# One critical section with hand-kept semaphores and a hardware loop on TensorE, in a batched A x B-transposed matmul

## Chip, cores and metric

The kernel runs on one core of one Trainium2 chip. The metric is the device time of one execution in microseconds (us). Nine runs of the kernel before have a median of 126.72 us, from 126.57 to 126.99 us.

## The reference

Sixteen independent products of a 512 x 512 matrix with the transpose of another, all in float32:

```python
batch, m, k, n = 16, 512, 512, 512
a: (batch, m, k) float32      b: (batch, n, k) float32
out = np.matmul(a, b.transpose(0, 2, 1)).astype(np.float32)
```

33.55 MB are read from HBM and 16.78 MB are written. TensorE (PE) contracts over the partition dimension, and both operands have k as their last dimension, so both must be turned before they can be multiplied.

## The kernel before

Batches are handled in pairs. Of a pair, 128 partitions hold the two batches, 64 partitions each; a partition holds eight consecutive rows of 512 floats, which is one run of 16 KB in HBM. J = 4 is the number of 128-row blocks of a batch, KO = 4 that of 128-wide blocks of k, HP = 64.

The work of a pair goes through five steps.

1. `load` (issued on SP's queue): one DMA for a and one for b, 2 MiB each (L56). The last pair is loaded in four DMAs of 1 MiB, batch by batch, in 8 KB runs (L50).
2. `halve`: VectorE (DVE) casts the loaded tile to bf16 in two pieces of 128 x 2048 (L64).
3. `turn_pair`: for each of the four ko, PE transposes eight 128 x 128 blocks into one PSUM tile `tp` by multiplying with an identity (L72). ScalarE (ACT) copies the a tiles to SBUF in two strided pieces (L78), DVE copies the b tiles in one (L85). All four ko of a come first, then all four of b; `tp` has four buffers. The last pair uses `turn_single` (L97, L102) batch by batch.
4. `multiply`: for each batch, four groups of four matmuls of 128 x 512 accumulate over ko in a PSUM tile `ps` (L111); ACT copies each to the output tile `o_sb` (L115).
5. `store`: one DMA of 1 MiB per batch on SP's queue (L122), in 8 KB runs.

The order is written out by hand: three pairs are loaded ahead; then, in the program of each engine, pair u's casts, transposes, matmuls and two stores are followed by the loads of pair u + 3. The framework places the semaphores that this order needs. SP's queue holds loads and stores in one line, so a store that waits for its output tile holds back the loads that stand behind it. PE's program is unrolled over all sixteen batches: 512 transposes and 256 matmuls, each with a weight load of its own.

Of the kernel before, what the change touches and what calls it, by code (L numbers as in the profile page):

```python
# [1 line left out]

# [5 lines left out]


@with_exitstack  # L10
def kernel(
    ctx: ExitStack,
    tc: tile.TileContext,
    a: bass.AP,
    b: bass.AP,
    out: bass.AP,
):
    nc = tc.nc
    P = 128
    batch, M, K = a.shape  # L20
    _, N, _ = b.shape
    J = M // P
    KO = K // P
    HP = P // 2
    f32 = mybir.dt.float32
    bf16 = mybir.dt.bfloat16
    AHEAD = 3

    const = ctx.enter_context(tc.tile_pool(name="ident", bufs=1))
    ident = const.tile([P, P], bf16)  # L30
    make_identity(nc, ident)

    apool = ctx.enter_context(tc.tile_pool(name="a_pool", bufs=3))
    bpool = ctx.enter_context(tc.tile_pool(name="b_pool", bufs=3))
    hpool = ctx.enter_context(tc.tile_pool(name="h_pool", bufs=3))
    tpool = ctx.enter_context(tc.tile_pool(name="t_pool", bufs=2))
    opool = ctx.enter_context(tc.tile_pool(name="o_pool", bufs=6))
    tppool = ctx.enter_context(tc.tile_pool(name="tp_pool", bufs=4, space=bass.MemoryType.PSUM))
    ppool = ctx.enter_context(tc.tile_pool(name="p_pool", bufs=4, space=bass.MemoryType.PSUM))

    def load(u, split):
        a_sb = apool.tile([P, 2 * J, K], f32, tag="a")
        b_sb = bpool.tile([P, 2 * J, K], f32, tag="b")
        if split:
            for e in range(2):
                for dst, src in ((a_sb, a), (b_sb, b)):
                    nc.sync.dma_start(  # L50
                        dst[:, e * J:(e + 1) * J, :],
                        src[2 * u + e].rearrange("(p j) k -> p j k", j=J),
                    )
        else:
            for dst, src in ((a_sb, a), (b_sb, b)):
                nc.sync.dma_start(  # L56
                    dst[:],
                    src[2 * u:2 * u + 2].rearrange("e (p j) k -> (e p) j k", j=2 * J),
                )
        return a_sb, b_sb  # L60

    def halve(src, e, tag):
        half = hpool.tile([P, J, K], bf16, tag="h" + tag)
        nc.vector.tensor_copy(out=half[:], in_=src[:, e * J:(e + 1) * J, :])  # L64
        return half

    def turn_pair(halves, is_a):
        turned = tpool.tile([P, KO, 2 * J * P], bf16, tag="ta" if is_a else "tb")
        for ko in range(KO):
            tp = tppool.tile([P, 2 * J, P], bf16, tag="tp")  # L70
            for j in range(2 * J):
                nc.tensor.transpose(  # L72
                    tp[:, j, :], halves[j // J][:, j % J, ko * P:(ko + 1) * P], ident[:]
                )
            if is_a:

                for e in range(2):
                    nc.scalar.copy(  # L78
                        out=turned[:, ko, e * J * P:(e + 1) * J * P].rearrange(
                            "k (j p h) -> k j p h", j=J, h=2  # L80
                        ),
                        in_=tp[:, :, e * HP:(e + 1) * HP].rearrange("k (h j) p -> k j p h", h=2),
                    )
            else:
                nc.vector.tensor_copy(  # L85
                    out=turned[:, ko, :], in_=tp[:].rearrange("k j p -> k (j p)")
                )
        return turned

    def turn_single(half, is_a):  # L90
        turned = tpool.tile([P, KO, J * P], bf16, tag="ta" if is_a else "tb")
        copy = nc.scalar.copy if is_a else nc.vector.tensor_copy
        for ko in range(0, KO, 2):
            tp = tppool.tile([P, 2, J * P], bf16, tag="tp")
            for h in range(2):
                for j in range(J):
                    nc.tensor.transpose(  # L97
                        tp[:, h, j * P:(j + 1) * P],
                        half[:, j, (ko + h) * P:(ko + h + 1) * P],
                        ident[:],  # L100
                    )
            copy(out=turned[:, ko:ko + 2, :], in_=tp[:])  # L102
        return turned

    def multiply(aT, bT, groups):

        o_sb = opool.tile([P, J, N], f32, tag="o")
        for j in range(J):
            ps = ppool.tile([P, N], f32, tag="p")
            for ko in range(KO):  # L110
                nc.tensor.matmul(  # L111
                    ps[:], aT(ko, j), bT(ko), start=(ko == 0), stop=(ko == KO - 1)
                )

            nc.scalar.copy(  # L115
                out=o_sb[:, j, :].rearrange("m (p j) -> m p j", j=groups),
                in_=ps[:].rearrange("m (j p) -> m p j", j=groups),
            )
        return o_sb

    def store(i, o_sb):
        nc.sync.dma_start(out[i].rearrange("(p j) n -> p j n", j=J), o_sb[:])  # L122

    pairs = batch // 2
    loaded = {}
    with tc.manual_schedule():
        for u in range(AHEAD):
            loaded[u] = load(u, u == pairs - 1)
        for u in range(pairs):
            a_sb, b_sb = loaded.pop(u)  # L130
            if u < pairs - 1:
                a_h = [halve(a_sb, e, "a") for e in range(2)]
                b_h = [halve(b_sb, e, "b") for e in range(2)]
                aT = turn_pair(a_h, True)
                bT = turn_pair(b_h, False)
                for e in range(2):
                    o_sb = multiply(
                        lambda ko, j: aT[:, ko, (e * J + j) * P:(e * J + j + 1) * P],
                        lambda ko: bT[:, ko, :].rearrange("k (j p) -> k j p", j=2 * J)[
                            :, :, e * HP:(e + 1) * HP  # L140
                        ],
                        2 * J,
                    )
                    store(2 * u + e, o_sb)
            else:
                for e in range(2):
                    a_h = halve(a_sb, e, "a")
                    b_h = halve(b_sb, e, "b")
                    aT = turn_single(a_h, True)
                    bT = turn_single(b_h, False)  # L150
                    o_sb = multiply(
                        lambda ko, j: aT[:, ko, j * P:(j + 1) * P],
                        lambda ko: bT[:, ko, :],
                        J,
                    )
                    store(2 * u + e, o_sb)
            if u + AHEAD < pairs:
                loaded[u + AHEAD] = load(u + AHEAD, u + AHEAD == pairs - 1)


# [1 line left out]
_INS = ['a', 'b']  # L162
_OUTS = [((16, 512, 512), 'float32')]


# [23 lines left out]
```

## Time and profile before

| | |
|---|---|
| median of 9 runs | 126.72 us (126.57 to 126.99) |
| profiled execution, its own time | 126.71 us |
| its span, first to last instruction | 124.9 us |
| granted TensorE clock, mean | 0.984 |
| busy: PE, weight loads, DVE, ACT | 94.3, 58.4, 58.7, 70.2 us |
| data on the DMA queues | 50.33 MB, 96.2% of 16 engines' span |
| HBM traffic over the span | 403 GB/s |

The page gives busy times of each engine over the span, and the span in 40 equal slices with a digit for the busy tenths of each; the DMA row is the mean busy share of 16 DMA engines, and GB/s is what they moved. "out<-in" names the tiles by the program's names. A group of instructions is told with its busy time, the mean of one, and the idle time of the engine ahead of it with what ended it. In the timeline the columns are the start, the duration, the engine and line, the operation, its tiles and shapes, the number of instructions and in brackets the idle time before. In the windows there stand, after the length, the busy time of each engine, the granted clock of PE, the DMA share and GB/s.

### The profile page before, as it was taken

The page shows a single profiled execution, that of the slowest core. Times are in us where ns is not written, and L with a number is a line of the kernel's source. Part 1 is how long each engine was busy: PE and PEld are TensorE (multiplying, and loading weights), DVE is VectorE, ACT ScalarE, POOL GpSimd, SP SyncE. Part 2 cuts the span into 40 slices and gives each one's busy share as a digit, 9 for nine tenths or more (in the row PEclk, how much of TensorE's full clock was granted, in tenths as well). Part 3 has the DMA queues.
Part 4 walks back from the last instruction along what each step waited for, and adds up shares of the span by engine and source line. Part 5 has one row for each costly group of instructions (what it writes and reads, how often), then busy time and mean ns, then how long its engine had stood idle before and what let it go on. Part 6 is the DMA issues. An engine that isn't in the chain of part 4 may idle for free.

```text
span 124.9 us, 1863 instructions
## 1 busy us (share of the span) xinstructions
PE 94.3 (75%) x768; PEld 58.4 (47%) x768; DVE 58.7 (47%) x64; ACT 70.2 (56%) x125; POOL 0.7 (1%) x6
## 2 busy tenths in 40 slices
PE   0007699997998899979956899278981999998910
PEld 0006494485447544844446346153460944747400
DVE  0034769617871761870738315482247664193100
ACT  4003904687569666946694367904679037859520
POOL 2000000000000000000000000000000000000000
PEclk9999999999999999999999999999999599999999
DMA  5999999999899999999999999999999999999954
GB/s 110 399 420 430 441 435 441 435 409 420 346 454 428 420 422 414 454 407 430 420 417 446 433 441 391 428 446 420 435 404 420 430 430 422 420 420 428 380 239 171
DMA packets 4904, 50.45 MB, mean 404 GB/s; under 512 B 544, under 2 KB 544, under 8 KB 544
## 3 DMA queue, kind: packets, MB, share of 16 engines
q1 hardware_dynamic: 4896, 50.33, 96.2%
q8 instruction: 6, 0.10, 0.3%
q14 instruction: 2, 0.02, 0.0%
HBM read 33.55 MB, written 16.78 MB: 403 GB/s over the span
## 4 chain that ended last, share of the span: by engine, by line
DMA 54%; PE 30%; DVE 7%; ACT 4%; SPq 1%; issue 1%
DMA b_sb<-in_b_dram 54%; PE ps L111 22%; PE tp L72 6%; DVE half L64 4%; ACT turned L78 2%; PE tp L97 2%; DVE turned L85 2%; ACT o_sb L115 1%; DVE turned L102 1%; SPq L56 1%; SPq L122 0%
## 5 line engine op out<-in xcount | busy, mean ns | idle before, releaser
L111 PE MATMUL ps<-turned 128*128 128x512 bf16 x256 | 58.8, 380 | 2.2 <-DVE turned L85 1.3
L115 ACT COPY o_sb<-ps 128x512 f32<-128x512 f32 x64 | 37.5, 586 | 38.7 <-PE ps L111 38.7
L72 PE MATMUL tp<-ident,half 128*128 128x128 bf16 x448 | 34.1, 238 | 22.6 <-DVE half L64 20.3
L72 PEld LDWEIGHTS <-half 128*128 128x128 bf16 x448 | 30.1, 107 | 27.2 <-DVE half L64 22.7
L111 PEld LDWEIGHTS <-turned 128*128 128x128 bf16 x256 | 24.9, 98 | 32.6 <-issue 5.5
L78 ACT COPY turned<-tp 128x512 bf16<-128x512 bf16 x56 | 28.1, 628 | 10.1 <-PE tp L72 10.1
L64 DVE CAST half<-a_sb 128x2048 bf16<-128x2048 f32 x16 | 19.0, 1222 | 23.6 <-DMA a_sb<-in_a_dram 23.6
L64 DVE CAST half<-b_sb 128x2048 bf16<-128x2048 f32 x16 | 19.0, 1224 | 16.9 <-DMA b_sb<-in_b_dram 16.9
L85 DVE COPY turned<-tp 128x1024 bf16<-128x1024 bf16 x28 | 18.5, 689 | 11.2 <-PE tp L72 11.1
L102 DVE COPY turned<-tp 128x1024 bf16<-128x1024 bf16 x4 | 2.6, 687 | 5.3 <-PE tp L97 5.3
L97 PEld LDWEIGHTS <-half 128*128 128x128 bf16 x64 | 3.7, 98 | 0.5
L97 PE MATMUL tp<-ident,half 128*128 128x128 bf16 x64 | 3.9, 219 | 0.0
L102 ACT COPY turned<-tp 128x1024 bf16<-128x1024 bf16 x4 | 3.9, 1015 | 0.0
L78 ACT ACT_TABLE_LOAD x1 | 1.3, 1283 | 0.7 <-PEq L173 0.7
masks.py:199 POOL TENSOR_SCALAR_AFFINE_SELECT ident<-ident 128x128 bf16<-128x128 bf16 x1 | 0.3, 292 | 0.1
masks.py:197 POOL MEMSET ident<- 128x128 bf16 x1 | 0.2, 205 | 0.3 <-POOLq L173 0.3
L173 POOL MEMSET const-bfloat16-1.0<- 128x1 bf16 x1 | 0.1, 102 | 0.0
L173 POOL MEMSET const-uint8-127<- 128x1 uint8 x1 | 0.1, 102 | 0.0
L173 POOL MEMSET const-float32-0.0<- 128x1 f32 x1 | 0.1, 98 | 0.2 <-issue 0.2
L173 POOL MEMSET const-float32-1.0<- 128x1 f32 x1 | 0.1, 98 | 0.0
## 6 DMA issues: line engine op xcount, KB each, us to landing
out_dram<-o_sb SPq DMA_DIRECT2D x16, 1024.0 KB, 18.1
a_sb<-in_a_dram SPq DMA_DIRECT2D x7, 2048.0 KB, 20.6
b_sb<-in_b_dram SPq DMA_DIRECT2D x7, 2048.0 KB, 25.0
a_sb<-in_a_dram SPq DMA_DIRECT2D x2, 1024.0 KB, 24.6
b_sb<-in_b_dram SPq DMA_DIRECT2D x2, 1024.0 KB, 24.7
```

The source lines that it names most:

```text
L56: nc.sync.dma_start(dst[:], src[2 * u:2 * u + 2].rearrange("e (p j) k -> (e p) j k", j=2 * J),)
L64: nc.vector.tensor_copy(out=half[:], in_=src[:, e * J:(e + 1) * J, :])
L72: nc.tensor.transpose(tp[:, j, :], halves[j // J][:, j % J, ko * P:(ko + 1) * P], ident[:])
L78: nc.scalar.copy(out=turned[:, ko, e * J * P:(e + 1) * J * P].rearrange("k (j p h) -> k j p h", j=J, h=2), in_=tp[:, :, e * HP:(e + 1) * H ...
L85: nc.vector.tensor_copy(out=turned[:, ko, :], in_=tp[:].rearrange("k j p -> k (j p)"))
L97: nc.tensor.transpose(tp[:, h, j * P:(j + 1) * P], half[:, j, (ko + h) * P:(ko + h + 1) * P], ident[:],)
L102: copy(out=turned[:, ko:ko + 2, :], in_=tp[:])
L111: nc.tensor.matmul(ps[:], aT(ko, j), bT(ko), start=(ko == 0), stop=(ko == KO - 1))
L115: nc.scalar.copy(out=o_sb[:, j, :].rearrange("m (p j) -> m p j", j=groups), in_=ps[:].rearrange("m (j p) -> m p j", j=groups),)
L173: nc = _bacc.Bacc("TRN2", target_bir_lowering=False, num_devices=1)
```

## The change

The framework's pools and ordering are replaced by one critical section in which each engine's program is written out with its own semaphores.

- Buffers: seven load slots of one tensor of a pair each (before, three for a and three for b), single bf16 buffers `ha`, `hb` and single turned buffers `ta`, `tb`, seven output tiles (before six), four `tp` and four `ps` in PSUM (as before).
- SP issues loads and stores in a fixed string `ORDER`, L for a load, S for a store. Loads from the eighth on wait until their slot's cast is done. All loads are of a pair, in 16 KB runs; the first a load is cut in two DMAs of 1 MiB, which split each partition's 16 KB run in two.
- ACT issues one store of 64 KB of zeros to part of out[0], early; the first real store waits until it has landed.
- PE runs eight turns of a hardware loop, one pair in each, laid at the head of an instruction block. Transposes of a and b alternate by ko. [...]each wait also takes the count off the semaphore again (`take`). The last pair is treated like the others.
- DVE and ACT do the same casts and copies as before, unrolled.

The new code, cut to its core:

```diff
+    NL = 7
+    NO = 7
+    ORDER = "LLLLLLSLLSLSSLSLLLSLSSLLSSSSSSSS"
...
+    with tc.tile_critical(no_gpsimd_drain=True):
...
+        for what in ORDER:
+            if what == "L":
+                u, slot = n_ld // 2, n_ld % NL
+                src = (a if n_ld % 2 == 0 else b)[2 * u:2 * u + 2].rearrange(
+                    "e (p j) k -> (e p) j k", j=2 * J
+                )
+                if n_ld >= NL:
+                    v = (n_ld - NL) // 2
+                    if (n_ld - NL) % 2 == 0:
+                        nc.sync.wait_ge(s_half, 2 * v + 2)
+                    else:
+                        nc.sync.wait_ge(s_tb, KO * v + 1)
+                if n_ld == 0:
+                    nc.sync.dma_start(ld[0][:, :J, :], src[:, :J, :]).then_inc(s_ld[0], 16)
+                    nc.sync.dma_start(ld[0][:, J:, :], src[:, J:, :]).then_inc(s_ld0, 16)
+                else:
+                    nc.sync.dma_start(ld[slot][:], src).then_inc(s_ld[slot], 16)
+                n_ld += 1
+            else:
+                slot = n_st % NO
+                if n_st == 0:
+                    nc.sync.wait_ge(s_warm, 16)
+                nc.sync.wait_ge(s_out, n_st + 1)
                 nc.sync.dma_start(
+                    out[n_st].rearrange("(p j) n -> p j n", j=J), ob[slot][:]
+                ).then_inc(s_st[slot], 16)
+                n_st += 1
...
+        for u in range(pairs):
+            for x, (h, s_c, s_t) in enumerate(((ha, s_ca, s_ta), (hb, s_cb, s_tb))):
+                n = 2 * u + x
+                landed = 16 * (n // NL + 1)
+                nc.vector.wait_ge(s_ld[n % NL], landed)
+                if u:
+                    nc.vector.wait_ge(s_t, KO * u)
+                nc.vector.tensor_copy(
+                    out=h[:, :J, :], in_=ld[n % NL][:, :J, :]
+                ).then_inc(s_half, 1)
...
+                nc.vector.tensor_copy(
+                    out=h[:, J:, :], in_=ld[n % NL][:, J:, :]
+                ).then_inc(s_c, 1)
+            for ko in range(KO):
+                nc.vector.wait_ge(s_tb, KO * u + ko + 1)
+                nc.vector.tensor_copy(
+                    out=tb[:, ko, :],
+                    in_=tp[:, (2 * ko + 1) % 4].rearrange("k j p -> k (j p)"),
+                ).then_inc(s_eb, 1)
...
+        nc.scalar.wait_ge(s_ld0, 16)
+        nc.scalar.dma_start(
+            out[0].rearrange("(p j) n -> p j n", j=J)[:, 0, :P], zero[:]
+        ).then_inc(s_warm, 16)
...
+        def take(s, n):
+            nc.tensor.wait_ge(s, n).then_inc(s, -n)
+
+        nc.tensor.wait_ge(s_set, 2)
+        with nc.Fori(
+            0, pairs, engines=[nc.tensor.engine], head_slot={nc.tensor.engine: 0}
+        ):
             for ko in range(KO):
+                for x, (h, s_c, s_t, s_e) in enumerate(
+                    ((ha, s_ca, s_ta, s_ea), (hb, s_cb, s_tb, s_eb))
+                ):
+                    if ko == 0:
+                        take(s_c, 1)
+                    if ko >= 2:
+                        take(s_e, 1)
+                    for j in range(2 * J):
+                        t = nc.tensor.transpose(
+                            tp[:, (2 * ko + x) % 4, j, :], h[:, j, ko * P:(ko + 1) * P],
+                            ident[:],
+                        )
+                    t.then_inc(s_t, 1)
+            take(s_ea, 2)
+            take(s_eb, 2)
+            for e in range(2):
+                for j in range(J):
+                    if e == 1:
+                        take(s_pv, 1)
+                    for ko in range(KO):
+                        t = nc.tensor.matmul(
...
+                    t.then_inc(s_mm, 1)
```

ACT's program, left out here, waits for `s_ta`, copies a `tp` tile to `ta` in the same two pieces as L78, and raises `s_ea`; then, for each `ps`, waits for `s_mm`, copies it as L115 does, and raises `s_pv` (the first three of the first batch and the first of the second) or `s_out` (with the last of a batch). From the eighth batch on it first waits until the output tile's earlier store has landed.

## The prediction

> **What bounds the kernel now.** I read the busy slices of the page first, then the chain that ended last, then the timeline of one pair, then the last windows.
>
> ```profile
> PE   0007699997998899979956899278981999998910
> DMA  5999999999899999999999999999999999999954
> GB/s 110 399 420 430 441 435 441 435 409 420 346 454 428 420 422 414 454 407 430 420 417 446 433 441 391 428 446 420 435 404 420 430 430 422 420 420 428 380 239 171
> q8 instruction: 6, 0.10, 0.3%
> ```
>
> The DMA row is full from the second slice to the 38th. A slice is 3.12 us; only the first and the last two run well under 420 GB/s. So the kernel is transfer-bound for some 115 us, and what can be won is at its two ends. PE is nearly full in slices 6 to 20 and has holes later. The first slice's 0.34 MB, at 424 GB/s, put the start of the stream at 2.3 us.
>
> ```profile
> 94.55 2.38 DVE half L64 x2
> 96.93 0.05 issue
> 96.97 3.15 PE tp L72 x28
> 100.12 7.20 PE ps L111 x32
> 107.32 1.35 PE tp L97 x24
> ...
> 113.23 1.35 PE tp L97 x24
> ...
> 115.95 3.20 PE ps L111 x14
> 119.14 0.02 issue
> 119.17 0.59 ACT o_sb L115
> ```
>
> The chain is one DMA until 94.5 us; from there it is compute, two late pairs back to back, up to the last eviction at 119.17 us. The last store is issued at 119.78 us.
>
> ```profile
> 112.50:118.70 6.20, 5.86 (x51) 3.53 (x50) 1.29 (x2) 4.48 (x7) 0.00 (x0) 1.00 0.97 404
> 118.70:121.80 3.10, 0.43 (x2) 0.00 (x0) 0.00 (x0) 0.77 (x2) 0.00 (x0) 1.00 0.56 235
> 121.80:124.90 3.10, 0.00 (x0) 0.00 (x0) 0.00 (x0) 0.00 (x0) 0.00 (x0) 0.91 0.42 172
> ```
>
> In the windows the last columns are DMA share and GB/s. The queues run partly dry at about 118.7 us while the last 1 MiB (1.05 MB) is not yet issued. It lands 4.1 us after its issue. The share of 0.56 before it moves says that some DMA engines still work off a backlog while the others wait: not all of the 3 us can be won.
>
> What PE costs when no load delays it is read from the early pairs:
>
> ```profile
> 37.78 2.44 PE L72 MATMUL tp<-ident,half 128*128 128x128 bf16 x40
> 38.49 4.01 ACT L78 COPY turned<-tp 128x512 bf16<-128x512 bf16 x8
> 43.56 6.42 PE L111 MATMUL ps<-turned 128*128 128x512 bf16 x29 [0.22 <-DVE turned L85]
> ```
>
> Stores start at 23.12, 35.14 and 47.17 us, so a pair takes **12.03 us** of PE: transposes paced by ACT's eight evictions (1.00 us per ko), then 32 matmuls at 6.42/29 = 0.221 us.
>
> [...]28 transposes take 3.10 us at 15.62 us and 3.15 us at 96.97 us (after idle times of 2.0 and 0.74 us), but 1.74 us at 82.10 us, after 2.46 and 0.74 us of idling.
>
> **The change, part by part.** Times are on the clock of the profiled execution (126.71 us with a span of 124.9 us: 1.8 us outside it; the median of the runs is 126.72 us, the same).
>
> *Start.* The first a load comes as two halves; the cast that PE waits for still ends at about 9.6 us, since s_ca is raised by the second half. a and b are now interleaved by ko, so only 8 transposes run before b is cast (13.21 + 2.37 = 15.6 us). 56 remain: 35 at 0.111 us[...], 21 at 1.74/28 = 0.062 us, to 20.8 us; the last evictions add 1.0 us and the matmuls 32 x 0.221 = 7.1 us. Pair 0 ends at 28.9, with waits 29.2 us, against 25.94 us before: **3.2 us later**. It need not reach the end: 12 MiB are queued at once, which keep the DMA busy to about 2.3 + 12.6 MB/424 GB/s = 32 us, and the first store is ready at 26.5 us.
>
> *A turn.* 0.7 us to the first eviction, 4 x 1.00 us of ACT, 0.15 us to the first matmul, 7.1 us of matmuls: 12.0 us, as before. Added: twelve waits that also decrement. The four on s_pv are met long before, and PE's queue covers them; eight lie in the transposes. SP's EVENT_SEMAPHOREs take 17 ns[...]. I take 0.04 us each, 0.35 us: **12.35 us**. The last s_pv wait is met when the first group of the second batch is evicted, 0.89 + 0.8 us into a batch of 3.5 us; the back edge follows some 1.8 us ahead of the array, so I cost it at nothing[...]. The last turn starts at 29.2 + 6 x 12.35 = 103.3 us.
>
> *Casts.* DVE's four (4.9 us a turn) now wait for the transposes of the turn before, since the bf16 buffers are single; they fit beside 7.1 us of matmuls. Nothing.
>
> *Loads.* Seven slots instead of six, and the last load is 40 MiB deep in the queue instead of 42. From the windows, 3.12 to 112.5 us moved 46.3 MB: 424 GB/s. 41.9 MB then end at 2.3 + 99.0 = 101.3 us. In the kernel before, the load that ends at the same depth was cast at 104.48 us, 3.2 us behind this line. Five of the six fetch blocks of PE go[...]; I take 2.5 us: cast begins at 103.8, ends at 106.2 us. So the load, not PE, is the later: 2.9 us.
>
> *Last pair.* From 106.2 us, b and a interleaved at ACT's pace: 4.3 us to the matmuls, 7.1 us, 0.8 us for the last eviction: the last store is ready at **118.4 us** against 119.78 us. **1.4 us** earlier.
>
> *Stores and SP.* Behind each wait of SP's for s_out stand the next loads. By the line of 2.48 us per MiB, S0 (26.5 us) is covered to 32 us, S2 and S3 (38.8, 42.3) to 52, S8 to S13 by far, S14 (114.8) to 116.1 us. Output slots come back far ahead (batch 14 needs the eighth store, landed near 92 us, at about 111). Nothing.
>
> *Small things.* 16 KB runs: seven of nine loads of each tensor had them, so a net 2 MiB changes; all-load slices run at 438, all-store ones (8 KB runs) at 422 GB/s, so at most 0.2 us. The 64 KB warm-up store: the slice with the first stores has 346 GB/s and the next gives back half; at most 0.35 us won, 0.2 us lost in short runs. ACT's and POOL's extra instructions lie under the first load. One entry and one exit of the section: unknown, -0.3 to +0.5 us; I take 0.
>
> *Sum.* The end moves with the last store, by 1.4 us. The stream alone would end at 2.3 + 50.4 MB/424 = 121.3 us plus about 1 us of stragglers, 122.3 us; the last store gives 118.4 + 3.8 = 122.2 us: both agree. 126.7 - 1.4 = **125.3 us**.
>
> **Rivals.**
> 1. *PE cools down before the last pair.* It idles from about 103.8 to 106.2 us. The trace shows both answers to such a hole. Cold, the 56 transposes take 5.2 + 0.9 instead of 4.3 us, 1.8 us more: store at 120.2 us, 127.1 us in all. Chance 0.15.
> 2. *PE becomes the bound: the slower side.* Its mechanism is the loop: waits that decrement[...] It decides from a turn of (119.78 - 0.8 - 29.2)/7 = **12.83 us**. At 13.5 us the last store is ready at 124.5 us: 131.4 us. For it: PE has no slack in the early pairs.[...] Chance 0.2.
> 3. *The fetches and not the last store were the bound:* loads land on the line and stragglers vanish; then the stream decides, 124.2 us. Chance 0.15.
> 4. *It doesn't do what it says for the time:* the backlog of single DMA engines stays, the load is cast at 104.5 us, the store is ready at 119.1 us and the end hardly moves: 126.3 to 126.9 us. Chance 0.12. The forecast has 0.38.
>
> **How the numbers follow.** Faster: 0.38 + 0.15 + 0.05 of rival 4 = 0.58; within 0.2% (what a measurement of this kernel can tell from no change): 0.10, from rivals 4 and 1; slower: 0.32. The range leaves out the worst half of rival 2 and a stream with no stragglers at all: 123.9 to 129.0 us; the forecast's own is 124.6 to 126.0 us.
>
> **What would show it.** Right: 16 KB instruction packets down from six to one or two; turns of 12.2 to 12.5 us between the first matmuls of early pairs; matmuls of pair 0 ending near 29 us; b of the last pair cast by 106 us; a last store issued near 118.4 us and a DMA row full one slice longer. Wrong: a turn over 12.8 us; packets on q8 once per turn; transposes at 0.11 us in the last turn; DMA slices under 400 GB/s in the middle, which would mean that SP's order leaves the queue dry.

## The result: slower by 0.7%, and the profile after

The changed kernel takes 127.62 us (median of 10 runs, 127.24 to 127.96), the kernel before beside it 126.73 us (31 runs, 126.53 to 127.05). The ratio is 1.0068, with a 95% interval from 1.0058 to 1.0078: **slower by 0.9 us**. 125.3 us was forecast, so the time moved the other way. The profiled execution took 127.86 us with a span of 126.09 us, against 126.71 and 124.92 us.

The rows of busy slices and the row of instruction fetches, from the page of the changed kernel:

```profile
PE   0003059699879969996995699969996991969910
DMA  4999999999799999999999999999999999999773
GB/s 91 400 439 437 426 426 416 447 447 385 299 455 405 437 408 465 387 426 447 392 444 405 437 421 437 408 434 398 426 447 431 431 398 429 429 421 416 312 309 130
q8 instruction: 1, 0.02, 0.0%
```

PE starts later and has a nearly empty slice (one tenth) at 104 to 107 us. Of six instruction packets of 16 KB (q8) one is left. In the GB/s row the dip at 31 us is deeper (299 GB/s, 346 before), and the row falls off one slice earlier.

Two early turns, from the timeline of the changed kernel (start, duration, engine and line, operation, number, idle time before):

```profile
23.49 7.07 PE L205 MATMUL ps<-tb,ta 128*128 128x512 bf16 x32 [0.96 <-PEq L175]
...
31.07 4.02 ACT L148 COPY ta<-tp 128x512 bf16<-128x512 bf16 x8
...
35.39 7.07 PE L205 MATMUL ps<-tb,ta 128*128 128x512 bf16 x32 [1.06 <-PEq L175]
```

ACT's eight copies take 4.0 us as before, and a turn takes 35.39 - 23.49 = 11.90 us, 0.13 us less than the unrolled 12.03 us. So no price of the loop is to be seen in a turn.

The last turn, from the same timeline:

```profile
103.72 0.61 PE L191 MATMUL tp<-ident,ha 128*128 128x128 bf16 x8
...
104.65 1.23 DVE L120 CAST hb<-ld 128x2048 bf16<-128x2048 f32 x1 [2.50 <-DMA ld<-in_b_dram]
...
107.16 1.01 PE L191 MATMUL tp<-ident,hb 128*128 128x128 bf16 x8 [2.82 <-PEq L175]
...
107.96 1.06 PE L191 MATMUL tp<-ident,ha 128*128 128x128 bf16 x8
...
113.03 7.07 PE L205 MATMUL ps<-tb,ta 128*128 128x512 bf16 x32 [1.05 <-PEq L175]
...
120.14 0.58 ACT L164 COPY ob<-ps 128x512 f32<-128x512 f32 x1 [0.28 <-PE ps L205]
120.75 0.33 SPq L105 DMA_DIRECT2D out_dram<-ob  x1
```

PE does the first eight transposes of a in 0.61 us and then waits 2.82 us for b. After that eight transposes take 1.0 us and more: **PE has cooled down**. From 107.16 to 110.4 us its transposes start every 107 ns at a granted clock of 0.50; after that they start every 56 ns, at 1.00. The last store is issued at 120.75 us, 1.0 us later than before. The chain that ended last holds no more than this turn's end, since it isn't followed past PE's waits:

```profile
113.03 7.08 PE ps L205 x32
120.11 0.02 issue
120.14 0.58 ACT ob L164
```

The last windows (length, busy times, granted clock, DMA share, GB/s):

```profile
112.50:118.70 6.20, 5.67 (x27) 2.63 (x28) 0.22 (x1) 3.45 (x7) 0.00 (x0) 1.00 0.85 357
118.70:121.80 3.10, 1.40 (x7) 0.43 (x5) 0.00 (x0) 1.47 (x3) 0.00 (x0) 1.00 0.74 307
121.80:126.10 4.30, 0.00 (x0) 0.00 (x0) 0.00 (x0) 0.00 (x0) 0.00 (x0) 0.77 0.52 213
```

More is left for these windows than before: (235 + 172) GB/s x 3.1 us = 1.26 MB after 118.7 us became 307 x 3.1 + 213 x 4.3 = 1.87 MB.

In the trace's packet records the last data packet ends at 124.25 us, 0.67 us later than before (123.58). From there to the end of the span it takes 1.83 us, before 1.34 us: 0.5 us more. Together these are the 1.17 us by which the span grew. The 0.5 us lie in the steps that close the program. There GpSimd clears the semaphores; first the row of the kernel before, then that of the changed one (number, duration in ns, start in us):

```profile
L184 POOLq EVENT_SEMAPHORE_RANGE_CLEAR  x1: 96/96/96, 124.5 to 124.5; - x1
```

```profile
L240 POOLq EVENT_SEMAPHORE_RANGE_CLEAR  x1: 222/222/222, 125.6 to 125.6; - x1
```

Ahead of it the changed kernel has a gathering of all engines, put down to the line that opens the section (L40); SP's waits in it:

```profile
L40 SPq EVENT_SEMAPHORE  x3: 17/28/28, 124.8 to 125.1; - x3
```

SP's last wait for a store ends at 124.71 us and GpSimd's first step of the program's end comes at 125.28 us, 0.57 us later; before, 124.14 and 124.27 us, 0.13 us. Gathering 0.44 us, clearing 0.13 us; SP's last wait follows the last packet 0.1 us sooner. At the other end, the first load is issued at 0.94 instead of 0.74 us, 0.2 us later.

### The profile page after: what moved, and what is told of

Its sections match the earlier page's. It is cut to its first block, busy times and chain, and to the rows that moved or that the text cites. A ratio compares the mean times of both kernels' runs of the same rounds, so it can differ in the third digit from the quotient of the medians.

```text
span 126.1 us, 1968 instructions
## 1 busy us (share of the span) xinstructions
PE 91.1 (72%) x768; PEld 57.9 (46%) x768; DVE 59.3 (47%) x64; ACT 71.0 (56%) x129; POOL 0.8 (1%) x7
## 5 line engine op out<-in xcount | busy, mean ns | idle before, releaser
L205 PE MATMUL ps<-tb,ta 128*128 128x512 bf16 x256 | 56.5, 379 | 8.4 <-PEq L175 8.4
L164 ACT COPY ob<-ps 128x512 f32<-128x512 f32 x64 | 37.5, 586 | 26.4 <-PE ps L205 26.4
L205 PEld LDWEIGHTS ps<-tb,ta 128*128 128x128 bf16 x256 | 24.5, 98 | 37.8 <-issue 9.5
L148 ACT COPY ta<-tp 128x512 bf16<-128x512 bf16 x64 | 32.9, 616 | 13.3 <-PE tp L191 13.3
L130 DVE COPY tb<-tp 128x1024 bf16<-128x1024 bf16 x32 | 22.1, 692 | 24.6 <-PE tp L191 24.6
L191 PE MATMUL tp<-ident,ha 128*128 128x128 bf16 x256 | 21.8, 234 | 10.9 <-PEq L175 10.9
L191 PE MATMUL tp<-ident,hb 128*128 128x128 bf16 x256 | 21.7, 233 | 9.7 <-PEq L175 9.7
L191 PEld LDWEIGHTS tp<-ident,ha 128*128 128x128 bf16 x256 | 17.9, 107 | 13.3 <-issue 10.9
L120 DVE CAST hb<-ld 128x2048 bf16<-128x2048 f32 x8 | 9.8, 1226 | 16.5 <-DMA ld<-in_b_dram 16.5
L120 DVE CAST ha<-ld 128x2048 bf16<-128x2048 f32 x8 | 9.8, 1221 | 10.0 <-DMA ld<-in_a_dram 10.0
L125 DVE CAST ha<-ld 128x2048 bf16<-128x2048 f32 x8 | 9.8, 1221 | 2.4 <-DMA ld<-in_a_dram 2.4
L125 DVE CAST hb<-ld 128x2048 bf16<-128x2048 f32 x8 | 9.8, 1220 | 0.0
```

The source lines that it names most:

```text
L120: nc.vector.tensor_copy(out=h[:, :J, :], in_=ld[n % NL][:, :J, :]).then_inc(s_half, 1)
L125: nc.vector.tensor_copy(out=h[:, J:, :], in_=ld[n % NL][:, J:, :]).then_inc(s_c, 1)
L130: nc.vector.tensor_copy(out=tb[:, ko, :], in_=tp[:, (2 * ko + 1) % 4].rearrange("k j p -> k (j p)"),).then_inc(s_eb, 1)
L148: c = nc.scalar.copy(out=ta[:, ko, e * J * P:(e + 1) * J * P].rearrange("k (j p h) -> k j p h", j=J, h=2), in_=tp[:, (2 * ko) % 4, :, e * ...
L164: c = nc.scalar.copy(out=ob[i % NO][:, j, :].rearrange("m (p j) -> m p j", j=2 * J), in_=ps[:, j, :].rearrange("m (j p) -> m p j", j=2 * J),)
L191: t = nc.tensor.transpose(tp[:, (2 * ko + x) % 4, j, :], h[:, j, ko * P:(ko + 1) * P], ident[:],)
```

## The experiments

All times are medians, all ratios stand against the kernel before on the same chip. "Last store" is its issue, "stream end" the end of the last data packet, both of the one profiled execution, whose own time stands ahead of them. It can lie away from the median: those of e2, e4, e7 and e8 are among the fastest of their runs, that of the changed kernel is 0.24 us above its median, and that of e13 is the slowest of its 13. Times are therefore compared by medians, and traces with the times of the profiled executions. Edits start from the changed kernel, where the kernel before isn't named.

The packet records don't name the DMA engine. But each DMA ends with 16 short completion packets (in the kernel before 544 packets of 4 bytes for 34 DMAs), which are read here as one from each of the 16 engines: the last 16 of a run show when its fastest and its slowest engine ended.

At the start two explanations stood against each other: that the end follows the last store (and so the cold PE or the late load), or that it follows the slowest of the DMA engines whatever the store does.

| | edit | us | ratio, 95% interval | profiled, us | last store | stream end |
|---|---|---|---|---|---|---|
| before | | 126.73 | | 126.71 | 119.78 | 123.58 |
| after | | 127.62 | 1.0068 (1.0058 to 1.0078) | 127.86 | 120.75 | 124.25 |
| e1_warm | PE kept busy in the last turn | 127.68 | 1.0068 (1.0042 to 1.0095) | 127.68 | 119.46 | 124.08 |
| e2_order | last two loads earlier | 127.24 | 1.0053 (1.0026 to 1.0079) | 127.04 | 116.16 | 123.45 |
| e3_before_pair_tail | before: last pair as a pair | 128.95 | 1.0167 (1.0138 to 1.0196) | 128.97 | 122.49 | 125.98 |
| e4_unrolled | no loop | 127.81 | 1.0093 (1.0061 to 1.0125) | 127.25 | 118.74 | 123.60 |
| e5_no_warm | e2 without zeros | 127.25 | 1.0043 (1.0024 to 1.0062) | 127.24 | 116.35 | 123.65 |
| e6_no_warm_ss | e5, other first stores | 127.39 | 1.0047 (1.0030 to 1.0063) | 127.59 | 116.72 | 124.00 |
| e7_before_loads_first | before: loads ahead of stores | 126.36 | 0.9973 (0.9958 to 0.9988) | 126.17 | 114.24 | 123.04 |
| e8_no_head | e2 without block alignment | 127.20 | 1.0046 (1.0029 to 1.0062) | 126.73 | 115.70 | 123.01 |
| e9_loads_first | e5, as e8, loads first | 127.37 | 1.0053 (1.0031 to 1.0075) | 127.36 | 120.23 | 123.73 |
| e10_before_section | before: section on GpSimd | 126.91 | 1.0018 (1.0006 to 1.0030) | 126.85 | 118.86 | 123.63 |
| e11_before_section_all | before: section on all engines | 130.54 | 1.0284 (1.0255 to 1.0313) | 130.69 | | |
| e12_no_split | e5, first load in one | 126.99 | 1.0019 (1.0003 to 1.0035) | 126.92 | 116.02 | 123.32 |
| e13_before_split | before: first load in two | 127.12 | 1.0031 (1.0019 to 1.0042) | 127.40 | 119.31 | 124.07 |
| e14_before_section_end | before: section at the end | 128.82 | 1.0171 (1.0156 to 1.0185) | 128.82 | 118.76 | 123.60 |

### Is it the cold PE? (e1_warm)

From the changed kernel: the last turn is taken out of the loop, and PE fills its wait for b with 44 transposes whose result is overwritten.

```diff
-        with nc.Fori(0, pairs, ...):
+        with nc.Fori(0, pairs - 1, ...):
+            turn(False)
+        turn(True)
...
+                        if last and x == 1:
+                            for r in range(44):
+                                nc.tensor.transpose(tp[:, 1, r % (2 * J), :], ha[:, r % (2 * J), :P], ident[:])
```

> The changed kernel with PE's last turn written out behind a loop of seven turns; in it 44 transposes of ha, whose results are overwritten, stand ahead of the wait for b's cast, so that PE doesn't idle there. Theory A (the end hangs on the last pair: its b load lands at 103.9 us, is cast by 107.0 us, and PE then transposes at half clock): b's first transpose to the first matmul falls from 5.9 to about 4.3 us, the last store is issued near 119.1 us instead of 120.7 us, time 126.0 us (127.62 us before this edit). Theory B (the transfer stream with its stragglers sets the end): the store is earlier but the time stays, 127.3 to 127.7 us.

From its timeline:

```profile
104.31 2.62 PE L186 MATMUL tp<-ident,ha 128*128 128x128 bf16 x44
107.33 0.61 PE L191 MATMUL tp<-ident,hb 128*128 128x128 bf16 x8 [0.40 <-PEq L175]
...
111.75 7.07 PE L205 MATMUL ps<-tb,ta 128*128 128x512 bf16 x32 [1.06 <-PEq L175]
```

PE is warm, eight transposes take 0.61 us, and the last store goes out 1.3 us earlier than in the changed kernel. The stream ends 0.17 us earlier and the time doesn't change: **the cooling is real, and taking it away wins nothing**. In the changed kernel all 16 engines end from 124.11 to 124.25 us. Here 15 end from 122.81 to 123.15 us, earlier with the store, and a single one ends at 124.08 us. So the end does not move with the last store.

### Is it the late load? (e2_order)

From the changed kernel: the last two loads are put ahead of the seventh and eighth store.

```diff
-    ORDER = "LLLLLLSLLSLSSLSLLLSLSSLLSSSSSSSS"
+    ORDER = "LLLLLLSLLSLSSLSLLLSLLLSSSSSSSSSS"
```

> The changed kernel with the last two loads moved ahead of the seventh and eighth store in SP's string, nothing else. They lie 36 to 38 MiB deep in the queue instead of 38 to 40. Theory A: the last b is cast near 100 to 102 us, before PE wants it at 103.7 us; PE runs its last turn without a hole, matmuls from 108.7 us, last store ready at 116.5 us; then the stream sets the end and the time is 125.3 to 126.0 us. Theory B: the same loads and stores in another order move the same bytes, 127.2 to 127.7 us.

The timeline of PE and the last windows:

```profile
106.77 0.61 PE L191 MATMUL tp<-ident,hb 128*128 128x128 bf16 x8
108.44 7.07 PE L205 MATMUL ps<-tb,ta 128*128 128x512 bf16 x32 [1.06 <-PEq L175]
```

```profile
112.50:118.70 6.20, 3.01 (x14) 1.18 (x12) 0.00 (x0) 2.52 (x5) 0.00 (x0) 1.00 1.01 427
118.70:121.80 3.10, 0.00 (x0) 0.00 (x0) 0.00 (x0) 0.00 (x0) 0.00 (x0) 0.74 0.87 367
121.80:124.90 3.10, 0.00 (x0) 0.00 (x0) 0.00 (x0) 0.00 (x0) 0.00 (x0) 0.50 0.06 26
```

No hole on PE is left, and the last store is issued 4.6 us earlier. The DMA share stays full until 118.7 us. Of the 4.6 us the stream's end gives back 0.8 us, as does the time of the profiled execution (127.86 to 127.04 us), which is the fastest of seven; the median gives back 0.4 us, which is no more than the intervals leave open. The share of 0.06 in the last window says why: hardly one of 16 engines still works. In the packet records the fastest engine ends at 120.89 us and the slowest at 123.45 us. The last landing is a matter of the **slowest DMA engine**, not of the last store.

### What was the split of the last pair worth? (e3_before_pair_tail)

From the kernel before: the last pair is loaded and multiplied like all others.

```diff
-            if u < pairs - 1:
+            if u < pairs:
...
-                loaded[u + AHEAD] = load(u + AHEAD, u + AHEAD == pairs - 1)
+                loaded[u + AHEAD] = load(u + AHEAD, False)
```

> The kernel before with its last pair loaded and handled as a pair like the others (no batch-by-batch loads, casts, transposes). Theory A: the last b lands whole at 42 MiB depth, near 108 us, and all of the last pair's b transposes and its 32 matmuls follow it: matmuls from about 115.5 us, last store ready near 123.4 to 125 us, time 130 to 132 us; so the batch-by-batch tail was worth 4 to 5 us, and the change gave it up. Theory B: under 1 us slower, 126.7 to 127.7 us.

From its PE timeline:

```profile
113.95 7.89 PE L111 MATMUL ps<-turned 128*128 128x512 bf16 x32
```

The matmuls of the last pair start at 113.95 us, the last store is issued 2.7 us later than before and the time rises by 2.1 us, to between what the two theories said. Here the last store does decide: all engines end within 0.14 us (125.84 to 125.98), 3.5 us behind its issue. So there are two regimes. After the changed kernel's store, too, the stream ends 3.5 us later (120.75 to 124.25 us). The slowest engine of the other runs ends at 123.0 to 124.1 us; less 3.5 us, that is 119.5 to 120.6 us. By this estimate a store later than that costs its delay; an earlier one finds the slowest engine still at work.

### Is it the loop? (e4_unrolled)

From the changed kernel: the eight turns are written out, with every `take` kept.

```diff
-        with nc.Fori(0, pairs, engines=[nc.tensor.engine], head_slot={nc.tensor.engine: 0}):
+        for u in range(pairs):
+            turn()
```

> The changed kernel with PE's loop unrolled in eight copies, waits that decrement kept. Theory A: the loop costs and brings nothing on the path (turns of 11.9 us already, under the 12.03 us of the kernel before): 127.3 to 127.9 us, though the fetch blocks on q8 come back to about six. Theory C (back edge and fetch cost something in each turn): faster by 1 us or more. Theory D (the saved fetch blocks bring something): slower by 0.5 us or more.

The page shows six packets on q8 again. The time is that of the changed kernel within the intervals, so no worth of the five saved fetches and of the loop shows either way. The PE timeline of its last turn:

```profile
103.21 0.61 PE L188 MATMUL tp<-ident,ha 128*128 128x128 bf16 x8
106.61 0.61 PE L188 MATMUL tp<-ident,hb 128*128 128x128 bf16 x8 [2.78 <-PEq L175]
107.05 0.61 PE L188 MATMUL tp<-ident,ha 128*128 128x128 bf16 x8
```

This hole is as long as the changed kernel's, 2.78 against 2.82 us, and here PE stays warm. The last store is issued at 118.74 us, 2.0 us earlier, and the stream ends 0.65 us earlier; this execution took 127.25 us, the fastest of five, whose median is no lower than the changed kernel's. It fits what e1 showed, if less sharply.

### The dip at the first stores (e5_no_warm, e6_no_warm_ss)

Both start from e2_order. The first drops the store of zeros and the waits for it; the second also sends the first two stores back to back.

```diff
-        nc.scalar.dma_start(out[0]...[:, 0, :P], zero[:]).then_inc(s_warm, 16)
...
-                if n_st == 0:
-                    nc.sync.wait_ge(s_warm, 16)
...
+    ORDER = "LLLLLLSSLLLSSLSLLLSLLLSSSSSSSSSS"   # the second only
```

> The changed kernel with the loads of e2_order and without the 64 KB store of zeros (so its output is unchanged). In e2_order the stream runs without a hole to 123.4 us and the time is 127.24 us. Theory E (the early store's short packets cost each DMA engine about 0.16 us and bring nothing; the slice with the first stores stays at 290 to 320 GB/s): 126.9 to 127.2 us. Theory F (the early store causes the deeper dip at the first stores, 299 against 346 GB/s before): the dip shrinks to the 346 GB/s of the kernel before and the time is 126.3 to 126.7 us. Theory G (the early store does help the first stores): slower, 127.5 us or more.

> As e5_no_warm, with the first two stores next to each other (LLLLLLSSLLL... instead of LLLLLLSLLSL...), as in the kernel before. Theory H (the dip at the first stores is deeper because loads follow directly on a single store): the slice of the first stores rises to about 346 GB/s and the time falls by 0.3 to 0.6 us against e5_no_warm. Theory E: no difference, within 0.2 us of e5_no_warm.

In the changed kernel the store of zeros moves in 128 packets of 512 bytes, 27 ns each: by an estimate from these, 128 x 27 / 16 ns = 0.2 us for each of 16 engines. The slice at 31 us has 319 and 320 GB/s, e2_order 314: the zeros neither cure nor cause the dip, and neither does the order of the first two stores. Times stay within 0.15 us of e2_order.

### The kernel before with its loads ahead of its stores (e7_before_loads_first)

From the kernel before: the loads of pair u + 3 are issued behind the casts of pair u instead of behind its stores.

```diff
                 b_h = [halve(b_sb, e, "b") for e in range(2)]
+                if u + AHEAD < pairs:
+                    loaded[u + AHEAD] = load(u + AHEAD, u + AHEAD == pairs - 1)
...
-            if u + AHEAD < pairs:
-                loaded[u + AHEAD] = load(u + AHEAD, u + AHEAD == pairs - 1)
```

> The kernel before with the loads of pair u + 3 moved ahead of the two stores of pair u on SP's queue, nothing else; the last load lies 40 instead of 42 MiB deep. Theory B (the slowest DMA engine has a backlog to 123.6 us in the kernel before, so an earlier last store wins nothing): the last store is issued near 117.5 us instead of 119.8 us, the DMA rows are full one slice longer, and the time stays, 126.4 to 126.9 us. Theory A, my prediction's (the last store sets the end): 124.5 to 125.2 us.

From its page, and its last windows:

```profile
DMA  5999999999999999999999999999999999999981
GB/s 105 400 432 427 427 427 448 437 427 422 427 422 427 369 424 445 416 435 408 437 440 427 408 422 445 422 427 416 429 419 429 422 424 422 422 427 427 429 358 47
```

```profile
118.70:121.80 3.10, 0.00 (x0) 0.00 (x0) 0.00 (x0) 0.00 (x0) 0.00 (x0) 0.50 0.74 314
121.80:124.90 3.10, 0.00 (x0) 0.00 (x0) 0.00 (x0) 0.00 (x0) 0.00 (x0) 0.50 0.04 19
```

**It beats both kernels**, by 0.27% with the interval clear of 1. The dip at 31 us is gone (427, 422 and 427 GB/s), a smaller one (369) stands at 42 us, and the last store is issued 5.5 us earlier than before (2.3 us earlier was expected). Again the gain is less than a tenth of that (0.37 us): the fastest DMA engine ends at 120.28 us, the slowest at 123.04 us. The edit changes the dip and the last store at once; which of them brings the gain wasn't separated.

### Instruction blocks, and more load lead (e8_no_head, e9_loads_first)

The first is e2_order without the alignment of the loop; the second adds e5's edit and an order that queues eight loads ahead of the first store.

```diff
-            0, pairs, engines=[nc.tensor.engine], head_slot={nc.tensor.engine: 0}
+            0, pairs, engines=[nc.tensor.engine]
...
+    ORDER = "LLLLLLLLSSLLSSLLSSLLSSLLSSSSSSSS"   # the second only
```

> The changed kernel with the loads of e2_order, PE's loop not laid at the head of an instruction block. Theory I (the one block that the loop head makes PE fetch at 5.8 us puts one DMA engine 1.1 us behind all others, and that engine ends the stream): the second half of the first load is cast near 8.8 instead of 9.6 us, and the time falls by 0.5 to 0.9 us, to 126.4 to 126.7 us. Theory K (there is always some engine that is 1.5 to 2.5 us behind, whichever it is): 127.0 to 127.4 us.[...]

> The changed kernel without the store of zeros, the loop not laid at a block's head, and SP's string LLLLLLLLSSLLSSLLSSLLSSLLSSSSSSSS: eight loads ahead of the first store, as e7_before_loads_first had them. Theory L (the stall at the first stores, about 1.0 us of each DMA engine between 28 and 40 us in all kernels with the section, 0.5 us in the kernel before and 0.1 us in e7, hangs on how long a store is queued before its turn): the dip in the slices at 31 us goes, the last packets end near 122.5 us, 126.4 to 126.8 us. Theory M (it belongs to the section's kernels whatever the order): the dip stays, 127.0 to 127.4 us. In both the last store is issued at about 116 us and the end of the program follows the last packet by 1.8 us instead of 1.3 us.

Without alignment the page shows no packet on q8 at all. The cast of the second half of the first a then starts 1.05 us earlier; first the row of e2_order, then that of e8_no_head:

```profile
9.65 1.23 DVE L125 CAST ha<-ld 128x2048 bf16<-128x2048 f32 x1 [2.31 <-DMA ld<-in_a_dram]
```

```profile
8.60 1.23 DVE L125 CAST ha<-ld 128x2048 bf16<-128x2048 f32 x1 [1.24 <-DMA ld<-in_a_dram]
```

In e2_order one 16 KB block is fetched at 5.91 us, while this load is in flight (the changed kernel: 5.83 us). e4_unrolled fetches six, but none before 32 us, and has the cast at 8.60 us too; e9_loads_first, with no fetch, at 8.58 us. So it is the early fetch that holds the load up. At the end nothing is left of that second (medians of 127.20 and 127.24 us).

In e9_loads_first the dip moves to 38 to 44 us with the first stores (365 and 321 GB/s in two slices), so it belongs to them and not to a time on the clock. Neither theory held whole: the dip left 31 us, as theory L had it, but the time is theory M's, and the last store is issued at 120.23 us where both had about 116 us. Its last load is 40 MiB deep in the queue again, as in the changed kernel, and the hole on PE is back; from its PE timeline:

```profile
106.73 0.61 PE L184 MATMUL tp<-ident,hb 128*128 128x128 bf16 x8 [3.20 <-PEq L168]
107.17 0.61 PE L184 MATMUL tp<-ident,ha 128*128 128x128 bf16 x8
107.62 0.82 PE L184 MATMUL tp<-ident,hb 128*128 128x128 bf16 x8
108.23 1.06 PE L184 MATMUL tp<-ident,ha 128*128 128x128 bf16 x8
```

PE comes out of 3.20 us of idling warm and turns cold about 1 us later.

### The section by itself (e10_before_section, e11_before_section_all, e14_before_section_end)

The kernel before, each time with one section that holds a GpSimd memset of 128x16. In the first it stands ahead of the loads; in the second every other engine also waits for the memset; in the third this stands behind the last store.

```diff
+    with tc.tile_critical(no_gpsimd_drain=True):
+        mark = ctx.enter_context(nc.sbuf_tensor("mark", [P, 16], f32))
+        s_mark = tc.alloc_semaphore("s_mark")                    # not in e10
+        nc.gpsimd.memset(mark[:], 0.0).then_inc(s_mark, 1)       # e10: no then_inc
+        for eng in (nc.sync, nc.scalar, nc.vector, nc.tensor):   # not in e10
+            eng.wait_ge(s_mark, 1)                               # not in e10
```

> The kernel before with an almost empty critical section (one memset on GpSimd) ahead of the loads, nothing else. Theory N (a section has a fixed price at its entry and exit: 0.20 us at the start and 0.65 us after SP's last wait in the trace of the changed kernel): all of it lies ahead of the first load here, whose issue moves from 0.74 to 1.4 to 1.7 us, and the time is 127.3 to 127.7 us. Theory O (the section's barriers overlap with other work): 126.7 to 127.0 us.

> The kernel before with a small critical section ahead of the loads in which all five engines take part (GpSimd writes a small tile, the four others wait for it), nothing else. e10_before_section had GpSimd alone in it: 126.91 us. Theory N (a section that all engines enter costs about 0.2 us at its entry and 0.4 to 0.6 us at its exit, in which SP gathers the other engines): the first load is issued 0.6 to 1.0 us later than 0.74 us and the time is 127.3 to 127.8 us. Theory O (the barriers cost nothing that other work doesn't hide): 126.7 to 127.0 us.

> The kernel before with a critical section of all five engines behind its last store: one GpSimd memset of 128x16 and a wait of every other engine for it. It prices the section's exit. If the exit costs what the trace of the changed kernel shows (0.5 us more between the last data packet and the end of the span than in the kernel before): 1.34 rises to 1.8-2.0 us, and with the section's own entry, memset and waits, which lie behind the last store's landing too if the section waits for it, to at most 2.5 us; time 127.2-127.9. Rival (the longer end of the changed kernel comes from the number of its semaphores, not from the section): the end stays within 0.15 us of 1.34 plus what the memset itself takes, time 126.6-127.0.

The first holds GpSimd alone, and SP's first load goes out at 0.74 us as before: its 0.2% is no price of a full section. The second measured something else than intended, as its timeline shows:

```profile
0.80 0.38 SPq L56 DMA_DIRECT2D a_sb<-in_a_dram  x1
8.91 0.11 POOL L129 MEMSET mark<- 128x16 f32 x1 [7.97 <-DMA a_sb<-in_a_dram]
...
9.38 0.33 SPq L56 DMA_DIRECT2D b_sb<-in_b_dram  x1
```

The framework put one load ahead of the section, which then waited for its landing; SP issued the next load at 9.38 us, and 3.8 us were lost. In the kernel before the second load is issued at 1.17 us: between these loads the section held it back by 8.2 us.

The third gives an upper bound of the price:

```profile
118.76 0.33 SPq L122 DMA_DIRECT2D out_dram<-o_sb  x1
124.65 0.11 POOL L163 MEMSET mark<- 128x16 f32 x1 [123.35 <-DMA out_dram<-o_sb]
```

The last packet ends at 123.60 us, as before, although the last store, with no edit ahead of it, went out 1.0 us earlier in this execution. From the last packet it takes 3.39 us instead of 1.34 us, and the time rises by the same 2.1 us. That is more than the changed kernel pays (0.5 us) and more than the 2.5 us that the expectation allowed at most. In its trace the way into the section and a second round of SP's waits for the stores (125.3 to 126.1 us) also lie behind the last landing. The rival, the number of semaphores, may hold for a part: the clearing takes 96, 138 and 222 ns in the kernel before, in this one and in the changed one.

What the changed kernel pays is plainer in the table. Profiled time less stream end is 3.59 to 3.72 us in all nine profiled executions of the changed kernel and its variants (after, e1, e2, e4, e5, e6, e8, e9, e12), and 2.99 to 3.33 us in the kernel before and its variants without a section of all engines (before, e3, e7, e10, e13).

### The cut of the first load (e12_no_split, e13_before_split)

e12_no_split is e5_no_warm with the first a load as one DMA. e13_before_split is the reverse: the kernel before with the cut, and nothing else. Theory Q is that the cut sets the DMA engines apart, so that they stall more when the first stores arrive.

```diff
+                if u == 0 and dst is a_sb:        # e13; e12 takes the same out
+                    nc.sync.dma_start(dst[:, :J, :], src[:, :J, :])
+                    nc.sync.dma_start(dst[:, J:, :], src[:, J:, :])
```

> As e5_no_warm (127.25 us) with the first load of a as one DMA of 2 MiB in 16 KB runs, as in the kernel before. Theory P (the split costs 128 more packets and one more DMA and wins nothing, since PE waits for both halves): 126.9 to 127.2 us. Theory Q (the split is what makes the stall at the first stores deeper): the slice of the first stores at about 31 us rises from 319 to about 346 GB/s and the time is 126.5 to 126.8 us. Theory R (no effect): within 0.15 us of e5_no_warm, dip as deep.

> The kernel before with one edit: the first a load is cut into two 1 MiB DMAs along the rows of each partition (8 KB runs), as the changed kernel cuts it. Theory Q (the cut load sets the 16 DMA engines apart, and they stall against each other when the first stores arrive): the 31 us slice falls from 346 to 300-330 GB/s, the time lost by an engine between 28 and 40 us rises from 0.49 to 0.8-1.0 us, and the time rises by 0.2-0.5 us, to 126.9-127.2. Rival (the stall belongs to the section's kernel and its order, and the cut load matters only there): slice and lost time stay within 15 GB/s and 0.1 us of before, time 126.6-126.9.

The rows of GB/s, of e5_no_warm, e12_no_split and e13_before_split in turn:

```profile
GB/s 89 410 452 418 434 423 428 439 439 366 319 441 421 454 405 447 394 421 449 413 444 436 434 423 423 421 447 426 439 418 413 428 426 423 428 428 428 423 277 13
```

```profile
GB/s 89 403 414 424 440 424 445 435 424 424 348 456 422 424 411 448 409 424 450 408 443 435 424 445 429 422 432 416 424 429 422 424 424 424 427 427 429 424 264 10
```

```profile
GB/s 102 392 452 439 428 423 439 428 418 392 347 447 428 428 420 413 449 434 428 400 418 452 423 439 387 436 431 444 420 410 426 420 434 420 420 434 415 358 339 50
```

Taken out of e5_no_warm, the cut frees the slice at 31 us (319 to 348 GB/s), as theory Q had it, and 0.26 us of the median, which is within the intervals and in the range of theory P. Put into the kernel before it costs 0.39 us, 0.31% with the interval clear of 1. But the 31 us slice stays at 347 GB/s: it is the slice ahead that falls, from 420 to 392. The time that packets of a DMA engine lost between 28 and 40 us, against 0.611 us for one of 16 KB and 0.309 us for one of 8 KB, averaged over the engines, is 0.49 us before and 0.78 us with the cut; 1.07 us in e5_no_warm and 0.49 us in e12_no_split. The other traces that start as the kernel before does (e3, e10, e14) have 0.42 to 0.55 us, so the cut does deepen the stall.

That this stall is what costs the time isn't shown. Summed over the whole stream by the same rule, an engine loses 2.24 us with the cut, and 1.97 to 2.39 us in before, e3, e10 and e14. And in the profiled execution of e13, the slowest of its runs, 15 engines end from 122.66 to 122.82 us and one alone at 124.07 us. The cost of the cut is shown by the runs; its way to the end of the program, and why a cut at 1 us is felt at 30 us, stay open.

## Why the prediction was wrong, by its own steps

**The step that failed.** "The end moves with the last store by 1.4 us", and with it the term "about 1 us of stragglers". The mechanism stood in rival 4 (the backlog of single DMA engines stays), with a chance of 0.12. In e2 the last store goes out at 116.16 us, earlier than the 118.4 us of the forecast, and the time is 127.24 us all the same. In all kernels with such an early last store (114.2 to 116.7 us) the stream still ends at 123.0 to 124.0 us. Against the prediction's 121.3 us for the stream the stragglers come to 1.7 to 2.7 us, not 1; behind the fastest engine (120.3 to 120.9 us) the slowest is by 2.1 to 3.3 us. In the packet records of the kernel before, one engine works without a break to 123.58 us, while most are idle for 1 to 3 us before the last store. With that engine at work an earlier store had nothing to win. The window with a DMA share of 0.56 pointed to it; the prediction read it as a warning, allowed about 1 us, and let the end follow the store all the same. The engines of one queue do not end together: in e7 the fastest ends at 120.28 us and the slowest at 123.04 us, 2.8 us apart.

**The forecast's own path.** In the changed kernel as it ran, the store came so late (120.75 us) that the end did follow it, and there the miss adds up from other terms. b's cast ended 0.8 us later than forecast, the way from it to the matmuls took 1.7 us more, that to the store 0.2 us less: 2.35 us at the store. From the store to the stream's end it took 3.5 instead of 3.8 us, and the end of the program 0.5 us more. 125.3 us become 127.86 us, the profiled execution's time. But e1 and e2 show that setting the first two terms right would not have brought 125.3 us.

**The start.** Pair 0 was to end at 29.2 us; its matmuls end at 23.49 + 7.07 = 30.56 us. Of the 1.4 us, 1.3 lie in b's first cast, which begins at 14.54 us instead of 13.21 us. The prediction had kept the old landing time of b. In e4 and e8, which fetch no block of instructions early, that cast begins at 13.54 and 13.56 us: 1.0 us is the block that the aligned loop fetches at 5.83 us. The prediction counted the blocks and didn't ask when they come. Its split of the 56 transposes behind b's cast, 35 slow and 21 fast, was an estimate: in the trace 43 of them start 107 ns apart, up to 21.7 us, and the rest 56 ns apart.

**A turn.** 12.35 us was forecast, 11.90 us measured. 0.35 us for twelve waits was too much as a lengthening of the turn: in the trace each is a row of 51 ns in PE's instruction stream, 96 in all, and the turn is shorter than before. What they cost alone wasn't measured, since e4 keeps them. Rival 2, the loop as the bound, does not occur. Its chance of 0.2 was an estimate. Nor does a stall at the back edge: q8 has one packet in the eight turns of the changed kernel and none in e8's. The branch itself takes 0.22 us in the trace, but it stands about 1.7 us ahead of the end of the turn's matmuls (28.88 against 30.56 us), close to the forecast's 1.8 us.

**Loads.** "I take 2.5 us: cast begins at 103.8"; it begins at 104.65 us, where the load of the same depth was cast in the kernel before (104.48 us). The saved fetch blocks bring no gain that e4 and e8 can show. No row of the trace had shown that they would; the step gave a lag of the loads a cause without one.

**Last pair.** 4.3 us from b's cast to the matmuls was forecast for a warm PE; from 107.01 to 113.03 us it was 6.0 us. Rival 1 had the mechanism and the size right (1.8 us) and set the store at 120.2 us; it is issued at 120.75 us. Its mechanism came true and, as e1 shows, taking it away wins nothing: the slowest engine ends as late without it.

**Splitting the last pair.** The kernel before won 2.1 us by it (e3). In the changed kernel the last pair's matmuls start at 113.03 us, 0.9 us ahead of e3's; with the last loads earlier, at 108.44 us (e2).

**Small things.** The zeros cost nothing, as forecast. Two terms at nothing were wrong. The cut of the first load, whose effect on the DMA engines the prediction didn't price at all, costs 0.39 us in the kernel before (e13); the 0.26 us of e12 are within the intervals. "Unknown, -0.3 to +0.5 us; I take 0" for the section was +0.5 us at its exit, the upper end of the range. The 16 KB runs were not tried by themselves.

**The sum from the runs.** From 127.62 us: last loads earlier, 127.24 us (e2); no zeros, 127.25 us (e5); no cut, 126.99 us (e12); the kernel before, 126.73 us. The last step fits the traces: e12's stream ends 0.26 us earlier than before, and its program's end is 0.48 us longer, 1.82 against 1.34 us. These single steps are no larger than their intervals; taken alone, only the cut is settled, by e13, and the 0.5 us at the program's end, by the traces.

## What to carry to other kernels

In a stream that keeps the DMA queues full, look at when each DMA engine ends, not only at when the last store is issued. Here one engine worked on while others idled, and a last store 4.6 us (e2) or 5.5 us (e7) earlier won 0.4 us. What won here was to leave the first load whole (0.39 us, e13) and to issue loads ahead of stores (0.37 us, e7); that both work through fewer stalls of the engines is likely, but not shown. The cost of leaving this section, 0.5 us between the last data packet and the end of the changed kernel's span, had no transfer left to hide behind; in e14, 2.1 us more there were 2.1 us more of time.

## What was unexpected in the hardware

- The 16 engines of one queue drift apart by 2.8 us over 50 MB (e7: 120.28 to 123.04 us), although each DMA ends with 16 completion packets (544 for 34 DMAs in the kernel before), read as one from each engine. What drives single engines back stays open.
- The first stores into a stream of loads cost a dip wherever they stand: 346 GB/s at 31 us before, 321 GB/s at about 42 us in e9, 369 GB/s at 42 us in e7.
- Whether PE cools in a wait is not told by its length alone: 2.82 us did it at once (after: the next eight transposes take 1.01 us, granted clock 0.50), 2.78 us didn't (e4: 0.61 us), 3.20 us did it about 1 us late (e9: 0.61 us, then up to 1.06 us). What decides it was not shown.
- Semaphores that are counted down at a wait, twelve in a turn and 51 ns each, didn't make the turn longer (11.90 us against 12.03 us).
- One block of instructions, fetched while the first load is in flight, puts that load's cast off by 1.05 us (e2: 9.65 us; e4 and e8: 8.60 us).
